# Attention scores over all 128 rows, two heads' scores in turn, and state space copies and tables in another order

## The chip, the cores and the metric

The kernel runs on one core of one Trainium2 chip. The metric is the device time of one launch in microseconds (us). Before the change the median of three runs is 2548.87 us (2544.2 to 2550.59).

## What is computed

One sequence of 512 positions with 1024 features, float32, goes through two layers of a first block and one layer of a second. Weights stay in float32, so every large product is done in split form: each operand is a high part and a low part, and a product is high·high + high·low + low·high.

The first block has three branches from one input projection: attention in a window of 128 positions (8 query heads, 2 key heads, 64 features a head, with sinks), a short convolution, and a state space model (32 groups of 16 channels, 64 states). The part of it that the change touches is this:

```python
s = jnp.einsum("bnqkgd,bnskd->bnkgqs", qb, kb) * (HEAD_DIM ** -0.5)
...
bu = jnp.einsum("blgh,gph->blgp", uf.astype(jnp.complex64), b_bar)
...
_, states = lax.associative_scan(combine, (a_elems, bu), axis=1)
...
y = jnp.einsum("blgp,ghp->blgh", states, c_c).real
```

The second block has a convolution branch with 31 taps and a differential attention: 8 heads, two causal softmaxes each, the second subtracted with a weight from the first.

```python
s = jnp.einsum('bqhd,bkhd->bhqk', qb, k, preferred_element_type=jnp.float32) * scale
s = jnp.where(mask[None, None], s, -jnp.inf)
...
a = probs(qb1, k1) - lam * probs(qb2, k2)
```

## The kernel before

**Storage and weights.** Intermediate tiles live in 78 slots of 128x512 that are handed out in the order in which they became free (`big` L338, `free` L352); the 8 PSUM banks are handed out the same way (`psum` L346). A tile that gets a slot waits until the last reader or writer of the tile before it is done, whatever engine that is. Weights come in units of 128x1024 through three raw buffers (`_fetch` L416), are split by ACT (high, L375) and DVE (low, L378) and are used in a fixed order. DMA requests go out on SP in program order. A product of eight such pieces is `fm` (L470), three matmuls a piece (`mm3` L457: lines L460, L461, L462).

**Lanes.** The main stream is a row of such products. Everything else is written as Python generators in lanes: after every third piece a tick gives each lane some steps (`beat` L464, `tick` L486), so pieces of attention, of the state space model and of the convolution are put between the main matmuls. Inside an engine the instructions then run in a fixed order.

**First block, attention** (`_att_block` L961). There are 4 query blocks and 2 key heads in each of 2 layers, so 16 calls. A call does four query heads, two for each half `e`. The keys stand twice in a tile of 128 rows, in rows 0 to 63 and in rows 64 to 127 (`kth` high, `ktl` low). The query tile `qs[e]` has the high part of the head in one half of the rows and its low part in the other half. So L976 over all 128 rows gives high·high + low·high, and L977 over the 64 rows of the high part adds high·low. L976 and L977 follow each other in turn, 4 of each in a call, 64 of each in all, into one bank; the scores are 256 columns wide, and 128 in the first query block.

**First block, state space model.** Four channel tiles `ct` in a layer. `ssm_tables` (L1093) builds the tables of one tile on POOL, for which it first asks for `bc` by a DMA (L1105); `ssm` (L1135) uses them on all engines and hands six slots back (L1223, L1224). L1102 holds a table back: those of tiles 0 and 1 until no table is outstanding, those of tiles 2 and 3 until at most one is. So table 1 is built only when tile 0 has used table 0. In layer 1 the first tables are started during the last products of layer 0. At the end of a tile, L1233 to L1242 bring the result from a PSUM bank into the slot `y` by 16 copies of 32x128: row block `i` of the output, and for each the four phases `t`, which stand in four row blocks of the bank and go to every fourth column. Copies of even `t` are ACT's (L375 in the profile), those of odd `t` DVE's (L1238).

**Second block, attention** (`_diff_block` L1654). There are 4 parts of 2 heads and 4 query blocks, 16 calls. `e` is the head of the part, and stands in one half of the 128 rows; `s` is the softmax. A call does, for each `e` and each `s`, three matmuls of 64 rows (`mm3` again: hence L460 to L462 with 64*128), a mask with its minimum on DVE (`masked` L532, L534) and an exponential on ACT. The scores are 128, 256, 384 or 512 columns wide by query block. There is a yield between the two heads. The calls go through a lane of width 2.

Of the kernel before, what the change touches and what calls it, by code (L numbers as in the profile page):

```python
# [11 lines left out]
AF = mybir.ActivationFunctionType  # L12
# [295 lines left out]
class Net:  # L308
# [652 lines left out]
    def _att_block(self, n, g, kth, ktl, qt, vv, ao, nsink, left, end):  # L961
        nc = self.nc
        while qt[n] is None:
            yield
        ts_ = slice(128 * n, 128 * n + 128)
        qs = qt[n][0]
        k0 = 1 if n == 0 else 0
        w = 256 - 128 * k0
        cols = slice(128 * (n - 1 + k0), 128 * (n + 1))
        nm = self.small("nm", (128, 4), bufs=3)  # L970
        pr = [self.big("pr", shape=(128, 2, 256)) for _ in range(2)]
        for e in range(2):
            ps = self.psum("sc", (128, 2, 256))
            rows = slice(64 * e, 64 * e + 64)
            for i in range(2):
                nc.tensor.matmul(ps[:, i, :w], qs[e][:, 2 * g + i], kth[g][:, cols], start=True, stop=False)  # L976
                nc.tensor.matmul(ps[:, i, :w], qs[e][rows, 2 * g + i], ktl[g][rows, cols], start=False, stop=True)  # L977
            for i in range(2):
                h = 2 * i + e
                self.masked(pr[i][:, e, :w], ps[:, i, :w], self.wmask[:, 128 * k0:], nm[:, h:h + 1],  # L980
                            nsink[:, 4 * g + h:4 * g + h + 1])
            self.free(ps)
        es = self.small("es", (128, 4), bufs=3)
        self.sub(es, nm, nsink[:, 4 * g:4 * g + 4])
        self.act(es, es, AF.Exp)
        sm = self.small("sm", (128, 4), bufs=3)
        for h in range(4):
            self.act(pr[h // 2][:, h % 2, :w], pr[h // 2][:, h % 2, :w], AF.Exp, scale=-1.0,
                     bias=nm[:, h:h + 1], accum_out=sm[:, h:h + 1])
        qt[n][1] -= 1  # L990
        if not qt[n][1]:
            self.free(qs)
        yield
        self.add(sm, sm, es)
        ri = self.small("ri", (128, 4), bufs=3)
        nc.vector.reciprocal(out=ri, in_=sm)
        for h in range(4):
            v = pr[h // 2][:, h % 2, :w]
            self.ts(v, v, ri[:, h:h + 1], ALU.mult)
        yield  # L1000
        pts = []
        for b in range(k0, 2):
            pt = self.psum("pT", (128, 4, 128))
            for h in range(4):
                nc.tensor.transpose(pt[:, h], pr[h // 2][:, h % 2, 128 * (b - k0):128 * (b - k0) + 128], self.ident)
            ph, pl = self.big("ph", F32R, (128, 4, 128)), self.big("pl", F32R, (128, 4, 128))
            self.split(ph, pl, pt)
            self.free(pt)
            pts.append((ph, pl, n - 1 + b))
        self.free(pr)  # L1010
        yield
        po = self.psum("po", (128, 4, 128))

        for i, (ph, pl, b) in enumerate(pts):
            v = vv[b // 2][:, b % 2, g].rearrange("p e d -> p (e d)")
            nc.tensor.matmul(po, v, ph, start=i == 0, stop=False)
            nc.tensor.matmul(po, v, pl, start=False, stop=i == len(pts) - 1)
            self.free(ph, pl)
        lo = self.big("lo", shape=(64, 4, 128))
        self.act(lo, po[64:128])  # L1020
        for h in range(4):
            rows = slice(64 * (h % 2), 64 * (h % 2) + 64)
            self.add(ao[2 * g + h // 2][rows, ts_], po[0:64, h], lo[:, h])
        self.free(po, lo)
        left[0] -= 1
        if not left[0]:
            end()
# [65 lines left out]
    def ssm_tables(self, L, ct, tabs):  # L1093

        gp = self.nc.gpsimd
        lr, li, fr, fi, rho, st = self.steps
        c4 = slice(4 * ct, 4 * ct + 4)

        def b4(ap, n):
            return ap[:, c4].unsqueeze(2).to_broadcast([128, 4, n])  # L1100

        while sum(t is not None for t in tabs.values()) > (1 if ct > 1 else 0):  # L1102
            yield
        bc = self.big("bc", shape=(128, 4, 4, 16))
        self.nc.sync.dma_start(out=bc, in_=self.A["bc"][L, ct].rearrange("p w (q h) -> p w q h", q=4))  # L1105
        bl = self.big("bl", shape=(128, 2, 4, 64))
        cl = self.big("cl", shape=(128, 2, 4, 64))

        def at(t, r, j):
            return t[:, r, j].rearrange("p (q h) -> p q h", q=4)  # L1110

        w1, w2 = self.small("s_w1", (128, 4, 16)), self.small("s_w2", (128, 4, 16))
        self.cmul(at(bl, 0, 3), at(bl, 1, 3), bc[:, 0], bc[:, 1], b4(fr, 16), b4(fi, 16), w1, w2, gp)
        for j in (2, 1, 0):
            self.cmul(at(bl, 0, j), at(bl, 1, j), at(bl, 0, j + 1), at(bl, 1, j + 1), b4(lr, 16), b4(li, 16), w1, w2, gp)
        pr, pi = bc[:, 2], bc[:, 3]
        for j in range(4):
            self.cmul(at(cl, 0, j), at(cl, 1, j), pr, pi, b4(lr, 16), b4(li, 16), w1, w2, gp)
            pr, pi = at(cl, 0, j), at(cl, 1, j)
        yield  # L1120
        er, ei, rt = (self.big(n, shape=(128, 4, 128)) for n in ("Er", "Ei", "R"))
        gp.memset(er[:, :, 0:1], 1.0)
        gp.memset(ei[:, :, 0:1], 0.0)
        gp.tensor_copy(out=rt, in_=b4(rho, 128))
        gp.memset(rt[:, :, 0:1], 0.0)
        xx = self.big("xx", shape=(128, 2, 4, 64))
        for k in range(7):
            n = 1 << k
            self.cmul(er[:, :, n:2 * n], ei[:, :, n:2 * n], er[:, :, 0:n], ei[:, :, 0:n],
                      b4(st[:, k, 0], n), b4(st[:, k, 1], n), xx[:, 0, :, :n], xx[:, 1, :, :n], gp)  # L1130
        self.free(xx)
        tabs[ct] = (bc, bl, cl, er, ei, rt)
        yield

    def ssm(self, L, ct, u, tabs, ys2):  # L1135
        nc = self.nc
# [16 lines left out]
        for i in range(4):  # L1153
            for j in range(4):
                o = uu[32 * j:32 * j + 32, i]
                s = u[32 * i:32 * i + 32, j::4]
# [16 lines left out]
        for r in range(2):  # L1173
            for e in range(2):
                s = hm[:, 2 * r + e:2 * r + e + 1]
# [5 lines left out]
        for r in range(2):  # L1181
            ps = self.psum("V", (128, 4, 128))
# [49 lines left out]
        y = self.big(f"y{ct}")  # L1232
        for i in range(4):  # L1233
            for t in range(4):
                o = y[32 * i:32 * i + 32, t::4]
                s = py[32 * t:32 * t + 32, i]
                if t % 2:
                    nc.vector.tensor_copy(out=o, in_=s)  # L1238
                else:
                    self.act(o, s)  # L1240
            if i == 1:
                yield  # L1242
# [3 lines left out]
        g = self.big("gelu")  # L1246
# [407 lines left out]
    def _diff_block(self, part, n, qk, vv, ya, left, done):  # L1654
        nc = self.nc
        while len(qk) < 4:
            yield
        w = 128 * (n + 1)
        tn = slice(128 * n, w)
        sm = self.small("dsm", (128, 2, 2), bufs=3)  # L1660
# [1 line left out]
        kap = self.small("dka", (128, 2), bufs=3)  # L1662
        ss = self.small("dss", (128, 2), bufs=3)
        rs = self.small("drs", (128, 2), bufs=3)
        pp = []
        for e in range(2):
            rows = slice(64 * e, 64 * e + 64)
            mx = self.small("dmx", (128, 2), bufs=4)
            p = [self.big("dp"), self.big("dp")]
            for s in range(2):  # L1670
                ps = self.psum("dsc")
                self.mm3(ps[:, :w], qk[s][0][rows, tn], qk[s][1][rows, tn],
                         qk[2 + s][0][rows, :w], qk[2 + s][1][rows, :w], True, True)
                self.masked(p[s][:, :w], ps[:, :w], self.cmask[:, 512 - w:], mx[:, s:s + 1])
                self.free(ps)
            for s in range(2):
                self.act(p[s][:, :w], p[s][:, :w], AF.Exp, scale=-1.0, bias=mx[:, s:s + 1], accum_out=sm[:, e, s:s + 1])
            pp.append(p)
            if e == 0:
                yield  # L1680
        nc.vector.reciprocal(out=ri, in_=sm)
        self.stt(kap, sm[:, :, 0], self.nlam, ri[:, :, 1], ALU.mult, ALU.mult)
# [1 line left out]
        for e in range(2):  # L1684
            p = pp[e]
# [133 lines left out]
```

## Time and profile before

| | |
|---|---|
| median of three runs | 2548.87 us |
| the profiled execution | 2549.26 us |
| its span, from the first to the last instruction | 2547.6 us |
| DVE busy | 1652.6 us (65%) |
| ACT busy | 1057.8 us (42%) |
| POOL busy | 333.7 us (13%) |
| mean granted clock of TensorE | 0.987 of full speed |

PE is TensorE's matmuls, PEld its weight loads, DVE VectorE, ACT ScalarE, POOL GpSimd, SP the engine that issues the DMAs. A matmul's duration in the rows holds its pipeline; what a matmul costs in a row of them is the distance between two starts. In the timeline the columns are the start, the duration, the engine, the line, the operation, the output from its inputs, the rows and columns of the weights, the shape of the moving operand, how many are merged, and in brackets the idle time of the engine just before and who ended it. In a table of stretches each row has the stretch, its length, the busy time of each engine with its instructions, the granted clock as a share of 2.4 GHz, the share of the DMA engines and what they moved. A clock of 0.50 is 1.2 GHz, the lower of its two levels.

### The profile page before, as it was taken

The numbers are of one execution on the slowest core, as the hardware profiler recorded it, in microseconds if no ns is written. First come the engines' busy times: TensorE is split into PE (matmuls) and PEld (weight loads), VectorE is DVE, ScalarE is ACT, GpSimd is POOL, SyncE is SP. The second block draws the span as 40 slices with busy tenths as digits, with TensorE's granted clock in tenths as the row PEclk, the third lists the DMA queues.
The fourth block names the chain that finished last, engine by engine and source line by source line (L and its number), as shares of the span: only waits on it lengthen the run. The fifth ranks groups of instructions, "written<-read, shape, count | busy, mean of one in ns | idle before, by whom it ended". The sixth has DMA issues, their size and how long they took to land. (4 is left out here: it accounts for less than half of the span.)

```text
span 2547.6 us, 32617 instructions
## 1 busy us (share of the span) xinstructions
PE 2478.0 (97%) x12280; PEld 2072.3 (81%) x12280; DVE 1652.6 (65%) x3086; ACT 1057.8 (42%) x1974; POOL 333.7 (13%) x826
## 2 busy tenths in 40 slices
PE   9999899999999999989999999999999989999997
PEld 7878788888888887878888788998888769988886
DVE  6887855444355488795577754689889776633445
ACT  5556543333233355553332222433444565633322
POOL 6554100000032074500000000000000000000001
PEclk9999999999999999999999999999999989999999
DMA  4211133222223311123366642333221113222322
GB/s 154 82 58 69 67 122 101 99 94 97 99 95 109 122 64 59 64 78 122 113 201 215 208 149 91 101 124 108 75 75 58 63 63 108 75 91 92 100 92 73
DMA packets 85566, 256.58 MB, mean 101 GB/s; under 512 B 9632, under 2 KB 13088, under 8 KB 85408
## 3 DMA queue, kind: packets, MB, share of 16 engines
q1 hardware_dynamic: 85408, 254.50, 29.4%
q8 instruction: 96, 1.57, 0.3%
q14 instruction: 62, 0.51, 0.1%
HBM read 248.18 MB, written 6.29 MB: 100 GB/s over the span
## 5 line engine op out<-in xcount | busy, mean ns | idle before, releaser
L460 PE MATMUL bank<-slot,wh 128*128 128x512 f32 x2680 | 1054.7, 395 | 14.7 <-ACT slot L375 10.1
L462 PE MATMUL bank<-slot,wl 128*128 128x512 f32 x2680 | 1050.3, 393 | 4.5 <-DVE wl L378 4.4
L461 PE MATMUL bank<-slot,wh 128*128 128x512 f32 x2680 | 1050.1, 392 | 0.0
L375 ACT ACTIVATE wh<-raw 128x1024 fp32r<-128x1024 f32 (+3 forms) x371 | 385.7, 1041 | 773.4 <-PE bank L461 480.4
L460 PEld LDWEIGHTS bank<-slot,wh 128*128 128x128 f32 x2680 | 506.7, 189 | 121.9 <-ACT slot L375 11.1
L462 PEld LDWEIGHTS bank<-slot,wl 128*128 128x128 f32 x2680 | 506.3, 189 | 115.9 <-DVE wl L378 8.1
L461 PEld LDWEIGHTS bank<-slot,wh 128*128 128x128 f32 x2680 | 506.6, 189 | 104.9 <-issue 0.9
L378 DVE TENSOR_TENSOR wl<-raw,wh 128x1024 fp32r<-128x1024 f32 (+3 forms) x371 | 451.6, 1218 | 184.4 <-ACT wh L375 181.8
L378 DVE TENSOR_TENSOR slot<-bank,slot 128x512 f32<-128x512 f32 (+4 forms) x340 | 198.3, 593 | 239.0 <-PE bank L462 209.1
L378 DVE TENSOR_TENSOR slot<-slot,slot 128x512 f32<-128x512 f32 (+4 forms) x492 | 295.0, 617 | 73.9 <-ACT slot L375 70.4
L375 ACT ACTIVATE slot<-slot 128x512 fp32r<-128x512 f32 (+4 forms) x384 | 207.9, 550 | 301.8 <-DVE slot L378 254.7
L375 ACT ACTIVATE slot<-bank 128x512 f32<-128x512 f32 (+7 forms) x388 | 177.1, 470 | 162.7 <-DVE slot L1238 47.3
L460 PE MATMUL bank<-slot,slot 128*128 128x256 f32 (+3 forms) x720 | 207.5, 298 | 3.1 <-ACT slot L375 3.1
L461 PE MATMUL bank<-slot,slot 128*128 128x256 f32 (+3 forms) x720 | 203.9, 290 | 3.7 <-DVE slot L378 3.7
L462 PE MATMUL bank<-slot,slot 128*128 128x256 f32 (+3 forms) x720 | 203.2, 288 | 0.0
L396 DVE SCALAR_TENSOR_TENSOR slot<-slot,slot 128x512 f32<-128x512 f32 (+1 forms) x184 | 125.5, 699 | 83.6 <-DMA slot<-in_wada_dram 59.2
L378 DVE TENSOR_TENSOR slot<-slot,bank 128x512 f32<-128x512 f32 (+1 forms) x112 | 68.4, 610 | 168.0 <-PE bank L462 167.2
L396 DVE SCALAR_TENSOR_TENSOR slot<-slot,cw,slot 128x493 f32<-128x493 f32 (+25 forms) x240 | 166.7, 733 | 1.6 <-ACT slot L375 0.9
L460 PEld LDWEIGHTS bank<-slot,slot 128*128 128x128 f32 (+1 forms) x720 | 135.6, 192 | 18.1 <-issue 7.1
L461 PEld LDWEIGHTS bank<-slot,slot 128*128 128x128 f32 (+1 forms) x720 | 136.3, 192 | 6.9 <-DVE slot L378 4.0
L462 PEld LDWEIGHTS bank<-slot,slot 128*128 128x128 f32 (+1 forms) x720 | 137.0, 192 | 1.3 <-issue 0.4
L461 PE MATMUL bank<-wl,slot 128*128 128x512 f32 (+1 forms) x256 | 93.6, 365 | 0.0
(189 smaller groups left out, 1944.6 us busy)
## 6 DMA issues: line engine op xcount, KB each, us to landing
raw<-in_w_dram SPq DMA_DIRECT2D x351, 512.0 KB, 3.3
slot<-in_wada_dram SPq DMA_DIRECT2D x96, 256.0 KB, 5.4
raw<-in_w_dram SPq DMA_DIRECT2D x48, 448.0 KB, 3.3
slot<-in_x_dram SPq DMA_DIRECT2D x16, 256.0 KB, 3.8
xd<-slot SPq DMA_DIRECT2D x16, 256.0 KB, 3.7
slot<-xd SPq DMA_DIRECT2D x16, 256.0 KB, 3.5
raw<-in_w_dram SPq DMA_DIRECT2D x9, 384.0 KB, 3.1
raw<-in_w_dram SPq DMA_DIRECT2D x8, 256.0 KB, 2.7
```

The source lines that it names most:

```text
L375: return self.nc.scalar.activation(out=out, in_=in_, func=func, scale=scale, **kw)
L378: return (eng or self.nc.vector).tensor_tensor(out=out, in0=a, in1=b, op=op)
L396: return self.nc.vector.scalar_tensor_tensor(out=out, in0=a, scalar=s, in1=b, op0=op0, op1=op1, **kw)
L460: t.matmul(ps, ah, bh, start=start, stop=False)
L461: t.matmul(ps, ah, bl, start=False, stop=False)
L462: t.matmul(ps, al, bh, start=False, stop=stop)
```

## The change

Four edits.

- In `_att_block` L977's product goes over all 128 rows, so that low·low is added as well.
- In `ssm_tables` all tiles have the same condition: a table may be built while one other is outstanding. This concerns table 1 alone.
- In `ssm` the 16 copies are dealt out by row block `i`: the four of blocks 0 and 2 to ACT, those of blocks 1 and 3 to DVE.
- In `_diff_block` the loops over head and softmax are exchanged: both heads of one softmax go together, into two banks, and their six matmuls alternate between the two halves of the rows. The masks of both come next, then the exponentials; the yield stands between the two softmaxes.

```diff
@@ _att_block
         for e in range(2):
             ps = self.psum("sc", (128, 2, 256))
-            rows = slice(64 * e, 64 * e + 64)
+
             for i in range(2):
                 nc.tensor.matmul(ps[:, i, :w], qs[e][:, 2 * g + i], kth[g][:, cols], start=True, stop=False)
-                nc.tensor.matmul(ps[:, i, :w], qs[e][rows, 2 * g + i], ktl[g][rows, cols], start=False, stop=True)
+                nc.tensor.matmul(ps[:, i, :w], qs[e][:, 2 * g + i], ktl[g][:, cols], start=False, stop=True)
@@ ssm_tables
-        while sum(t is not None for t in tabs.values()) > (1 if ct > 1 else 0):
+        while sum(t is not None for t in tabs.values()) > 1:
             yield
@@ ssm
-                if t % 2:
+                if i % 2:
                     nc.vector.tensor_copy(out=o, in_=s)
                 else:
                     self.act(o, s)
@@ _diff_block
-        pp = []
-        for e in range(2):
-            rows = slice(64 * e, 64 * e + 64)
-            mx = self.small("dmx", (128, 2), bufs=4)
-            p = [self.big("dp"), self.big("dp")]
-            for s in range(2):
-                ps = self.psum("dsc")
-                self.mm3(ps[:, :w], qk[s][0][rows, tn], qk[s][1][rows, tn],
-                         qk[2 + s][0][rows, :w], qk[2 + s][1][rows, :w], True, True)
-                self.masked(p[s][:, :w], ps[:, :w], self.cmask[:, 512 - w:], mx[:, s:s + 1])
-                self.free(ps)
-            for s in range(2):
-                self.act(p[s][:, :w], p[s][:, :w], AF.Exp, scale=-1.0, bias=mx[:, s:s + 1], accum_out=sm[:, e, s:s + 1])
-            pp.append(p)
-            if e == 0:
+
+        pp = [[self.big("dp"), self.big("dp")] for _ in range(2)]
+        mx = [self.small("dmx", (128, 2), bufs=4) for _ in range(2)]
+        for s in range(2):
+            ps = [self.psum("dsc") for _ in range(2)]
+            for i, (x, y) in enumerate(((0, 0), (0, 1), (1, 0))):
+                for e in range(2):
+                    rows = slice(64 * e, 64 * e + 64)
+                    nc.tensor.matmul(ps[e][:, :w], qk[s][x][rows, tn], qk[2 + s][y][rows, :w], start=i == 0, stop=i == 2)
+            for e in range(2):
+                self.masked(pp[e][s][:, :w], ps[e][:, :w], self.cmask[:, 512 - w:], mx[e][:, s:s + 1])
+            self.free(ps)
+            for e in range(2):
+                v = pp[e][s][:, :w]
+                self.act(v, v, AF.Exp, scale=-1.0, bias=mx[e][:, s:s + 1], accum_out=sm[:, e, s:s + 1])
+            if s == 0:
                 yield
```

## Rows read from the trace of the kernel before

**Rows 1.** The page's first part: the span, and TensorE's busy time.
```profile
span 2547.6 us, 32617 instructions
PE 2478.0 (97%) x12280; PEld 2072.3 (81%) x12280; DVE 1652.6 (65%) x3086; ACT 1057.8 (42%) x1974; POOL 333.7 (13%) x826
```

**Rows 2.** Busy time by stage: first block's two layers, plain products, second block's attention.
```profile
60.00:268.00 208.00, 199.70 (x984) 163.14 (x984) 162.69 (x368) 116.44 (x267) 109.09 (x290) 0.97 0.20 68
900.00:1105.00 205.00, 188.94 (x922) 154.36 (x920) 164.28 (x343) 117.07 (x272) 108.33 (x291) 0.95 0.19 63
1536.00:1600.00 64.00, 64.00 (x284) 53.01 (x283) 28.64 (x36) 18.73 (x24) 0.00 (x0) 1.00 0.30 95
1792.00:2035.00 243.00, 240.06 (x1273) 192.97 (x1272) 205.76 (x442) 117.53 (x287) 10.33 (x10) 1.00 0.19 64
2035.00:2180.00 145.00, 130.08 (x793) 111.18 (x792) 101.82 (x234) 90.64 (x222) 7.55 (x10) 0.94 0.27 93
```

**Rows 3.** The same table, of the stretches in which PE stands still.
```profile
150.00:180.00 30.00, 26.21 (x96) 19.26 (x96) 22.02 (x55) 14.98 (x36) 13.13 (x30) 0.83 0.15 52
256.00:280.00 24.00, 17.93 (x81) 14.31 (x80) 21.80 (x34) 11.68 (x28) 7.72 (x16) 0.86 0.13 44
970.00:1000.00 30.00, 23.86 (x94) 17.75 (x94) 23.83 (x55) 14.54 (x35) 10.85 (x21) 0.89 0.16 54
1088.00:1112.00 24.00, 15.88 (x88) 13.99 (x85) 22.10 (x38) 14.05 (x31) 0.10 (x1) 0.79 0.19 66
```

**Rows 4.** Line L976's matmuls: count and shapes.
```profile
L976 PE MATMUL bank<-slot,slot x64: 220/382/582, 82.5 to 1020.5; 128*128 128x256 f32 x48, 128*128 128x128 f32 x16
```

**Rows 5.** Timeline of PE in a call of the first block's attention.
```profile
122.47 0.38 PE L977 MATMUL bank<-slot,slot 64*128 64x256 f32 x1
...
123.10 0.38 PE L977 MATMUL bank<-slot,slot 64*128 64x256 f32 x1
```

**Rows 6.** Timeline of PE around three 64-row score groups, 256, 512 and 128 wide.
```profile
1815.36 0.28 PE L462 MATMUL bank<-slot,slot 128*128 128x256 f32 x1
...
1816.33 0.28 PE L461 MATMUL bank<-slot,slot 128*128 128x256 f32 x1
...
2006.60 0.39 PE L462 MATMUL bank<-slot,wl 128*128 128x512 f32 x1
...
2008.15 0.40 PE L461 MATMUL bank<-slot,wh 128*128 128x512 f32 x1
...
1800.35 0.40 PE L462 MATMUL bank<-wh,slot 128*128 128x512 f32 x1
1800.68 0.33 PE L461 MATMUL bank<-slot,slot 64*128 64x128 f32 x1
1800.69 0.32 PE L460 MATMUL bank<-slot,slot 64*128 64x128 f32 x1
...
1801.51 0.40 PE L461 MATMUL bank<-wl,slot 128*128 128x512 f32 x1
```

**Rows 7.** Timeline of ACT and POOL: the waits around tables 1 and 2.
```profile
89.60 0.29 POOL L378 TENSOR_TENSOR s_w<-slot,s_fr 128x64 f32<-128x64 f32 x1 [31.44 <-DMA slot<-in_bc_dram]
157.63 0.63 ACT L375 ACTIVATE slot<-slot 128x512 fp32r<-128x512 f32 x1 [5.70 <-POOL slot L378]
905.89 0.29 POOL L378 TENSOR_TENSOR s_w<-slot,s_fr 128x64 f32<-128x64 f32 x1 [60.42 <-DMA slot<-in_bc_dram]
979.41 0.63 ACT L375 ACTIVATE slot<-slot 128x512 fp32r<-128x512 f32 x1 [7.73 <-POOL slot L378]
```

**Rows 8.** Waits of ACT (total us, times, longest), and PE's longest idle time.
```profile
ACT slot L375 <- DVE slot L1238: 58.1, 47, 5.6
...
1099.10 0.56 PE L1228 MATMUL bank<-slot,slot 128*128 128x128 f32 x1 [8.12 <-DVE slot L1238]
```

**Rows 9.** A long wait of POOL for a slot; SP's waits at line L1105.
```profile
671.24 0.10 POOL L1123 MEMSET slot<- 128x4 f32 x1 [195.54 <-PE bank L461]
...
SPq L1105 <- DVE slot L378: 31.1, 3, 13.5
```

## The prediction

> **What bounds the kernel now.** The first part of the page says it at once: TensorE's matmuls are busy for 2478.0 of 2547.6 us, 97% [rows 1]. Busy is not yet at its peak, so the next view is the busy time by stage [rows 2]. A stage of plain products has 284 matmuls of 512 columns in 64 us, 0.225 us each at full clock; that is the pace to hold everything against (256 columns cost half, 0.113 us). The change touches four other stages: the first block's layers from 60 to 268 and from 900 to 1105 us, and the second block's attention from 1792 to 2035 and on to 2180 us. In the first three PE is busy for 96, 92 and 99% of the time, and DVE, the next engine, for 78, 80 and 85%. So a PE microsecond taken out there should mostly shorten the run, with not very much room before DVE is next. From 2035 to 2180 us PE is busy for 90% only: there chains of small steps set the pace too.
>
> Then I looked for where PE stands still in these stages. There are four patches [rows 3], two in each layer. PE is idle for 3.8, 6.1, 6.1 and 8.1 us in them, in order of time, and the granted clock falls to the lower of its two levels for part of each: a mean of 0.83 over 30 us is 10.2 us at half speed, of which at most 3.8 were idle, so 3.2 to 5.1 us of work are lost on top. Done likewise for the others, the patches cost 7.0 to 8.9 (150 to 180 us), 6.4 to 9.4 (256 to 280), 6.4 to 9.4 (970 to 1000) and 9.1 to 13.1 us (1088 to 1112).
>
> **First edit: first-block scores over 128 rows.** No matmul comes or goes; one in two grows from 64 to 128 rows. What to see: L976 and L977 in turn start 0.63 us apart for two, 0.315 us each [rows 5], where 256 columns cost 0.113 in a plain row [rows 2]. The pair changes the number of rows at each step, and each step pays. There are 64 of each line, 48 of them 256 wide [rows 4]. If all run on 128 rows, the 96 wide ones save 0.202 us each, 19.4 us. For the 32 narrow ones I read no distance and take half that saving, 3.2 us. Together 22.6 us, in equal parts in the two layers; more is excluded, as the plain pace is the floor, and the least is 0, if DVE takes the time up. Masks, exponentials, banks and weight loads are as many as before, so nothing new waits. I take three quarters, **17 us**, since the masks on DVE must keep up with an engine that is already at 78 to 80%.
>
> **Second edit: table 1 earlier.** The work on POOL is the same; it moves. Now POOL is idle for 31.4 us before 89.6 us and for 60.4 us before 905.9 us, both times until the `bc` of table 1 has landed, and then it builds tables 1 and 2 one after the other; some 68 and 74 us later an instruction at the head of ACT's queue, a split into a slot that POOL still works on, is let go after 5.7 and 7.7 us [rows 7]. That is the first patch of each layer: PE runs out of what ACT should have given it. With one table outstanding allowed, table 1 is built in the gap before (in layer 1 as early as layer 0's last products). A table is half of 74, 37 us of POOL. Table 2 may still start only where tables 1 and 2 start now, so POOL is done some 30 us sooner, before ACT's split arrives, and both waits should go. At stake are 7.0 to 8.9 plus 6.4 to 9.4, so 13 to 18 us, and the bounds are 0 and 18. What is late next there is DVE (22.0 of 30 us busy, [rows 3]), so I take **12 us**. What the move issues elsewhere: POOL's 37 us fall beside products in which DVE is little loaded (28.6 of 64 us in such a stage [rows 2]), which costs nothing as long as that cover lasts; two `bc` requests go ahead of weight requests on SP, at nothing as long as their slots are free (a rival, below). Table 3 still waits for tile 1 and stays where it is.
>
> **Third edit: copies by row block.** Still 8 copies on each engine. Now each is let go by the one before it on the other engine: ACT waits 47 times for L1238, 58.1 us in all, and PE's longest idle time, 8.12 us, ends on L1238 [rows 8]. Whatever else DVE has in its queue between two copies delays ACT, and with it the weight splits behind. In runs of four, 15 handovers become at most 3. The patches at stake are the second of each layer, 6.4 to 9.4 plus 9.1 to 13.1, middle 19 us; but they are the end of a chain through all engines, of which the copies are one link, and table 3 another. So the bounds are 0 (the chain ends as late) and 19 (the copies were all of it). I take the runs of four to follow each other rather than to overlap, because in the rows every copy waits, those of other row blocks too, and put in **7 us**. The Trainium skill (PSUM — Partial Sum Buffer, PSUM bank collisions raise a hardware error) says that two engines may be in one bank together only in different quadrants of 32 partitions. By that rule the old order, which changed the quadrant at each copy, could have overlapped and the new one can't, so this edit would give nothing and the sum would be 43 instead of 50; the 47 waits show that the old order did not overlap either.
>
> **Fourth edit: both heads in turn.** 192 matmuls of 64 rows, 64 groups of three now, 32 groups of six then. A group of three costs, from the last plain start before it to the second plain start behind it and less two plain distances, 0.97 - 0.226 = 0.74 us at 256 columns and 1.55 - 0.45 = 1.10 us at 512 [rows 6]; for 384 I take the middle, 0.92. This counts the extra start on the way in and out. What do six in turn cost? The kernel before shows it by chance: at 1800.68 and 1800.69 us two matmuls of different halves start together, and six of them, the groups of both heads at 128 columns, take 1.16 - 0.45 = 0.71 us [rows 6], no more than three at 256. So I take six for the price of three: 8 groups saved at each of three widths, 8 x (0.74 + 0.92 + 1.10) = 22 us; at 128 columns nothing, since some of these overlap already. The upper bound is 22; the lower is 0, if each change of half costs what rows 5 show for a change of rows: six at 0.33 are 2.0 us, two groups at 512 are 2.2. About two thirds of it lie before 2035 us, where PE is the bound, one third in the stage behind. I take three quarters of the first and two fifths of the second, **14 us**. Two banks are held at a time instead of one after the other, and freed in the same step; the banks go round in the same order, so I cost that at nothing, as long as the masks of both heads follow at once. The exponentials of the first head now stand behind the second head's mask: one mask later, in a lane of two calls, hidden by the main products.
>
> **The sum.** 17 + 12 + 7 + 14 = 50 us off the profiled execution's own 2549.3 us (span 2547.6 [rows 1], 1.7 around it; 0.4 above the median of the runs): **2499 us**. With every term in full, 22.6 + 18 + 19 + 22 = 82 us, it would be 2468.
>
> **The rivals.**
> - *DVE becomes the bound.* It stands at 78 to 85% in the stages and its queue has a fixed order. If no stage gets over the highest share seen, 85%, the stages end at 162.7/0.85 = 191, 164.3/0.85 = 193 and 205.8/0.85 = 242 us: 17 + 12 + 1, and 2 from the last stage, 32 us in all: 2517 us. For it: DVE's shares [rows 2]. Against it: it is 90% busy and more in the short patches [rows 3], and short waits there are not its own work. Chance 0.22.
> - *Everything lands.* The clock no longer falls, PE is the bound throughout: about 78 us, 2471 us. For it: PE at 96 and 99%. Against it: four patches would have to vanish. Chance 0.14.
> - *The halves don't overlap.* Then the fourth edit gives its lower bound, 0 instead of 14: 2513 us. The pair at 1800.68 speaks against it. Chance 0.05.
> - *The copies give nothing.* The runs of four still follow each other and the chain's end hangs on table 3: 0 instead of 7, 2506 us. For it: POOL still builds table 3 late. Against it: the 47 waits [rows 8]. The page's rule above would end here. Chance 0.05.
> - *Slower: SP stops on a table's slot.* The request for `bc` of table 1 now stands on SP ahead of weight requests, and SP does nothing else until its slot is free. Three raw buffers cover three units of 24 matmuls, 16 us. A longer stop stands in PE's time at full price, so one of over 16 + 50 = 66 us makes the kernel slower; of 100 us, 2499 + 84 = 2583 us. For it: a slot that POOL wanted at this very place, while layer 0 ends, came free 195.5 us late [rows 9]. Against it: the waits at L1105 so far are three, 13.5 us at most [rows 9], and the oldest free slot is taken first. Chance 0.06.
>
> **How the numbers follow.** My forecast has 0.45, with a range of its own from 2485 to 2512. The remaining 0.03 is for a kernel in which the gains cancel against new waits. Left out of 2475 to 2530 are the slower case, the cancelled gains and half of the case in which everything lands: under 0.2. A measurement can tell about 0.3%, 8 us, from no change. All cases but the last two are faster by more than that; a tail of the DVE case is not: faster 0.89, same 0.04, slower 0.07.
>
> **What would show it.** First edit: L976 and L977 both on 128 rows, starts about 0.12 us apart. Second: POOL busy soon after 58 us in layer 0 and before 905 us in layer 1, no wait of ACT for POOL near 155 and 975 us, and the granted clock at 1.00 in the first patch of each layer. Third: L1238's copies in runs of four, ACT's waits for them far below 58 us, PE idle less around the second patches. Fourth: starts of 64-row matmuls in pairs, and six in the time of three. I am wrong if DVE is idle less than before for the same gain (the first rival), if a request at L1105 holds SP up for more than 16 us, or if the 64-row starts stay 0.2 us and more apart.

## The result, and the profile after

The changed kernel takes **2515.82 us** (median of 4, 2514.38 to 2516.97) against 2548.20 of the kernel before on the same chip: a ratio of 0.9874, 95% interval 0.9857 to 0.9891, so 32 us less (28 to 36). The forecast was 2499, in a range from 2475 to 2530: the sign and the range held, the sum of 50 us was too large by a third of itself. The profiled execution took 2516.28 us.

The page's first part answers to [rows 1]: the share of TensorE rises by a point, DVE is no busier than it was.

```profile
span 2514.5 us, 32649 instructions
...
PE 2451.9 (98%) x12280; PEld 2065.7 (82%) x12280; DVE 1642.0 (65%) x3086; ACT 1056.9 (42%) x1974; POOL 331.1 (13%) x826
```

The table by stage (duration; busy time of PE, PEld, DVE, ACT, POOL; granted clock; DMA share; GB/s) answers to [rows 2]. DVE is at 84, 83 and 84% in the first three.

```profile
60.00:268.00 208.00, 198.63 (x1031) 168.61 (x1029) 174.84 (x388) 123.36 (x285) 105.86 (x270) 0.98 0.20 68
900.00:1105.00 205.00, 195.73 (x1012) 167.42 (x1011) 170.53 (x352) 123.01 (x280) 67.21 (x182) 0.98 0.20 68
1792.00:2035.00 243.00, 230.88 (x1198) 184.48 (x1197) 203.84 (x437) 129.66 (x320) 11.57 (x13) 0.97 0.19 65
2035.00:2180.00 145.00, 140.65 (x953) 126.59 (x952) 100.99 (x232) 88.59 (x218) 5.88 (x8) 0.98 0.28 97
```

Fixed windows mislead once the work inside them has moved. So I laid the start of the same plain matmul in the two traces side by side. Of the matmuls that use a split weight (`wh` or `wl`) the 1080th starts at 328.3 us before and 313.7 after: layer 0 gave 14.6. The 4320th, behind layer 1, starts 33.5 earlier (1141.4 and 1108.0): layer 1 gave 18.9. For the matmul at 2182.8, behind the second block's attention, it is 33.8 (2149.0 after). **All of the gain comes from the first block; the second block's attention gave nothing.**

What became of each edit shows in four places. First edit: L977 has 128 rows, and the four starts of a call are 0.12 us apart, as against 0.315 in [rows 5] (timeline of PE).

```profile
126.26 0.28 PE L977 MATMUL bank<-slot,slot 128*128 128x256 f32 x1
126.38 0.28 PE L976 MATMUL bank<-slot,slot 128*128 128x256 f32 x1
126.50 0.28 PE L977 MATMUL bank<-slot,slot 128*128 128x256 f32 x1
```

Second edit: the waits of [rows 7] are gone, and with them the first patch of each layer. PE is busy throughout there, at a clock of 1.00, where [rows 3] have 0.83 and 0.89 (table by window).

```profile
150.00:180.00 30.00, 30.00 (x159) 25.43 (x158) 26.85 (x71) 20.75 (x49) 0.00 (x0) 1.00 0.26 88
...
970.00:1000.00 30.00, 30.00 (x152) 25.41 (x151) 24.63 (x69) 23.02 (x55) 0.00 (x0) 1.00 0.21 71
```

But ACT now waits for POOL elsewhere, and PE stands still right behind two of these waits (timeline of ACT; in brackets the idle time before, and what ended it).

```profile
65.64 0.91 ACT L375 ACTIVATE slot<-slot,cst 128x256 f32<-128x256 f32 x2 [4.88 <-POOL slot L378]
...
119.73 0.91 ACT L375 ACTIVATE slot<-slot,cst 128x256 f32<-128x256 f32 x2 [6.61 <-POOL slot L378]
...
918.90 0.91 ACT L375 ACTIVATE slot<-slot,cst 128x256 f32<-128x256 f32 x2 [7.62 <-POOL slot L378]
```

PE idles 2.33 us before 122.05 and 3.40 before 924.19; that ACT's wait is behind it is read from the times, since the row names DVE. In layer 0 POOL now works on tables 0 and 1 in turn, an instruction of one and then of the other, so table 0 is done later: the wait at 65.64 is for it. A table has 16 instructions of the form `slot<-s_w,s_w`, and the last one for table 0 ends at 70.15 instead of 57.30. The two longer waits are for the third table in POOL's order, table 2: its last such instruction ends 0.04 us before ACT starts, at 119.69 (in layer 1 at 918.87). Before, it ended at 163.83 (timeline of POOL, before and after):

```profile
163.51 0.32 POOL L378 TENSOR_TENSOR slot<-s_w,s_w 128x64 f32<-128x64 f32 x1
...
119.38 0.31 POOL L378 TENSOR_TENSOR slot<-s_w,s_w 128x64 f32<-128x64 f32 x1
```

So that table is done 44 us sooner, but ACT's instruction behind it comes sooner too: the ninth of its form (`slot<-slot,cst`, 128x256) was the 177th of all that ACT does and is now the 124th. In all ACT waits 45.9 us for slots that POOL works on at L378; before it was 41.2. At 124 us of the kernel before, the changed kernel is 3.1 us *behind*.

Third edit: the copies run in fours, and DVE's begin where ACT's end, at 250.85 us. ACT's waits for them fall from 58.1 us, 47 times [rows 8], to 20.4 us, 13 times (timeline of ACT and DVE). The other link of the chain in layer 0 stays: just ahead of these copies ACT waits 7.76 us for POOL, and PE idles 5.34 us before 256.16.

```profile
249.27 1.58 ACT L375 ACTIVATE slot<-bank 32x128 f32<-32x128 f32 x4
...
250.88 1.58 DVE L1238 COPY slot<-bank 32x128 f32<-32x128 f32 x4 [5.45 <-ACT slot L375]
```

Fourth edit: the source now alternates the heads, the chip does not. TensorE still gets three matmuls of one head, then other work, then three of the other (timeline of PE). At 256, 384 and 512 columns this holds for nearly every group; at 128 some alternate, as some did before [rows 6].

```profile
1814.56 0.96 PE L1673 MATMUL bank<-slot,slot 64*128 64x512 f32 x3
...
1816.95 0.79 PE L1673 MATMUL bank<-slot,slot 64*128 64x384 f32 x3
...
1820.49 0.96 PE L1673 MATMUL bank<-slot,slot 64*128 64x512 f32 x3
```

The order of an engine's instructions is laid out when the program is built; of what the source issues in a row, the build may put the instructions apart, and here it kept each bank's three together.

### The profile page after: what moved, and what is told of

Its sections match the earlier page's. It is cut to its first block, busy times and chain, and to the rows that moved or that the text cites. A ratio compares the mean times of both kernels' runs of the same rounds, so it can differ in the third digit from the quotient of the medians.

```text
span 2514.5 us, 32649 instructions
## 1 busy us (share of the span) xinstructions
PE 2451.9 (98%) x12280; PEld 2065.7 (82%) x12280; DVE 1642.0 (65%) x3086; ACT 1056.9 (42%) x1974; POOL 331.1 (13%) x826
## 4 chain that ended last, share of the span: by engine, by line
PE 79%; DVE 6%; POOL 5%; DMA 5%; ACT 2%; issue 2%; SPq 0%; POOLq 0%; DVEq 0%; ACTq 0%
PE bank L460 25%; PE bank L461 24%; PE bank L462 24%; DMA slot<-in_wada_dram 4%; POOL slot L378 3%; POOL s_w L378 2%; DVE slot L378 2%; DVE wl L378 2%; ACT slot L375 2%; DVE slot L396 1%; PE bank L1673 1%; DMA raw<-in_w_dram 1%; PE bank L1705 1%; PE bank L1005 0%; PE bank L1184 0%
## 5 line engine op out<-in xcount | busy, mean ns | idle before, releaser
L460 PE MATMUL bank<-slot,wh 128*128 128x512 f32 x2680 | 1053.7, 394 | 13.1 <-ACT slot L375 7.7
L378 DVE TENSOR_TENSOR wl<-raw,wh 128x1024 fp32r<-128x1024 f32 (+3 forms) x371 | 451.1, 1216 | 189.3 <-ACT wh L375 186.0
L378 DVE TENSOR_TENSOR slot<-bank,slot 128x512 f32<-128x512 f32 (+4 forms) x340 | 197.7, 592 | 233.3 <-PE bank L462 199.9
L378 DVE TENSOR_TENSOR slot<-slot,slot 128x512 f32<-128x512 f32 (+4 forms) x492 | 292.1, 611 | 56.5 <-ACT slot L375 53.6
L375 ACT ACTIVATE slot<-bank 128x512 f32<-128x512 f32 (+6 forms) x388 | 176.9, 471 | 132.7 <-PE bank L462 47.9
L462 PE MATMUL bank<-slot,slot 128*128 128x256 f32 x656 | 184.8, 285 | 0.0
L461 PE MATMUL bank<-slot,slot 128*128 128x256 f32 x656 | 184.7, 286 | 0.0
L460 PE MATMUL bank<-slot,slot 128*128 128x256 f32 x656 | 183.2, 288 | 0.3 <-ACT slot L375 0.3
L378 DVE TENSOR_TENSOR slot<-slot,bank 128x512 f32<-128x512 f32 (+1 forms) x112 | 68.3, 610 | 168.3 <-PE bank L462 167.5
L396 DVE SCALAR_TENSOR_TENSOR slot<-slot,cw,slot 128x485 f32<-128x485 f32 (+28 forms) x240 | 166.3, 728 | 1.9 <-ACT slot L375 1.1
L460 PEld LDWEIGHTS bank<-slot,slot 128*128 128x128 f32 x656 | 124.7, 194 | 2.4 <-ACT slot L375 1.2
L461 PEld LDWEIGHTS bank<-slot,slot 128*128 128x128 f32 x656 | 125.9, 193 | 0.9 <-issue 0.4
L462 PEld LDWEIGHTS bank<-slot,slot 128*128 128x128 f32 x656 | 126.2, 193 | 0.4
L583 POOL TENSOR_TENSOR rstd<-nv,mhalf 128x2 f32<-128x2 f32 (+1 forms) x11 | 10.5, 953 | 634.4 <-DVE nv L393 634.4
```

The costliest lines, as they stand in the source:

```text
L375: return self.nc.scalar.activation(out=out, in_=in_, func=func, scale=scale, **kw)
L378: return (eng or self.nc.vector).tensor_tensor(out=out, in0=a, in1=b, op=op)
L396: return self.nc.vector.scalar_tensor_tensor(out=out, in0=a, scalar=s, in1=b, op0=op0, op1=op1, **kw)
L460: t.matmul(ps, ah, bh, start=start, stop=False)
L461: t.matmul(ps, ah, bl, start=False, stop=False)
L462: t.matmul(ps, al, bh, start=False, stop=stop)
```

## The experiments

**Each edit alone, on the kernel before** (the kernel before took 2551.65 us beside these four, and each gain below is one less the ratio, times that).

```diff
-nc.tensor.matmul(ps[:, i, :w], qs[e][rows, 2 * g + i], ktl[g][rows, cols], start=False, stop=True)
+nc.tensor.matmul(ps[:, i, :w], qs[e][:, 2 * g + i], ktl[g][:, cols], start=False, stop=True)
```

> The first edit alone, on the kernel before. Theory: a change of row count costs PE about 0.2 us at each step and PE is the bound here, so the 96 wide score matmuls give 0.2 us each: 15 to 20 us less, about 2530 us, half of it in each layer. Rival (the stage's end hangs on the chain through POOL's tables and DVE's copies, which this edit does not touch): the scores come earlier and wait longer, 10 us less at most, and the idle time of PE at 155 and 975 us grows by what the scores save.

Measured: 2531.78 us, ratio 0.9919 (0.9906 to 0.9932): 20.7 us less (17 to 24); in the trace 9.9 in layer 0 and 8.8 in layer 1. The theory holds. Of the rival a part is true: PE's idle time does grow, at 155 us from 2.69 to 5.23 and near 970 us from 6.13 to 9.53 (timeline of PE), so the scores do come early and wait; but most of the saving of 0.2 us each is kept for all that.

```profile
158.80 0.58 PE L976 MATMUL bank<-slot,slot 128*128 128x256 f32 x1 [5.23 <-DVE slot L378]
...
967.49 0.79 PE L1016 MATMUL bank<-slot,slot 128*128 128x512 f32 x1 [9.53 <-ACT slot L375]
```

```diff
-while sum(t is not None for t in tabs.values()) > (1 if ct > 1 else 0):
+while sum(t is not None for t in tabs.values()) > 1:
```

> The second edit alone, on the kernel before. Theory: table 1 is built between the pieces of table 0, so the waits of ACT for POOL near 155 and 975 us go, but waits of 5 to 8 us come 40 us earlier, at about 65, 120 and 919 us: the wait has moved, and the gain is 2 to 8 us, 2540 to 2546 us. Rival (the changed kernel's gain in the layers comes mainly from here, as predicted): 12 us less, 2536 us, and no wait over 3 us in either layer.

Measured: 2545.87 us, 0.9976 (0.9967 to 0.9985): 6.1 us less (4 to 8). The theory holds: the wait has moved. At 126 us this kernel is 6.0 us behind the kernel before, and only by 173 us is it 2.2 ahead.

```diff
-if t % 2:
+if i % 2:
```

> The third edit alone, on the kernel before. Theory: the handovers go, PE's idle time at the end of each layer shrinks by what the copies held it, 3 to 8 us less, 2540 to 2545 us. Rival (the end of the chain hangs on table 3 and on DVE, the copies are hidden): within 2 us of the kernel before, though ACT's waits for the copies fall from 58 to about 20 us.

Measured: 2551.20 us, 0.9994 (0.9984 to 1.0005): 1.5 us less, no change that can be told. ACT's waits for the copies did fall, to 23.4 us, 14 times, as the rival said: alone, the copies are hidden behind tables and scores that are late anyway.

```diff
-self.mm3(ps[:, :w], qk[s][0][rows, tn], qk[s][1][rows, tn],
-         qk[2 + s][0][rows, :w], qk[2 + s][1][rows, :w], True, True)
...
+for i, (x, y) in enumerate(((0, 0), (0, 1), (1, 0))):
+    for e in range(2):
+        rows = slice(64 * e, 64 * e + 64)
+        nc.tensor.matmul(ps[e][:, :w], qk[s][x][rows, tn], qk[2 + s][y][rows, :w], start=i == 0, stop=i == 2)
```

> The fourth edit alone, on the kernel before. Theory: the build issues the three matmuls of one head together, whatever order the source has, so TensorE does what it did: within 2 us of the kernel before, 2546 to 2550 us, groups of three at 0.74 to 1.1 us as before. Rival (two banks held at a time and the exponentials behind the second head's mask cost or give something): over 4 us in either direction, from 1792 us on.

Measured: 2547.23 us, 0.9986 (0.9978 to 0.9995): 3.6 us less (1 to 6). Of that the trace shows 1.5 behind 1792 us; the rest lies ahead of any line that the edit touches. So this is close to nothing, as expected. The four gains add up to 31.9 us; all together gave 32. That they agree so well is partly chance: most of the 3.6 us is not the edit's, and the third edit is worth more in company, as the next run shows.

**The changed kernel less one edit.**

```diff
-if i % 2:
+if t % 2:
```

> The changed kernel without the third edit (copies by column again). Theory: the copies are worth 1 to 2 us as they were alone, 2516 to 2518 us. Rival (with the other edits in, the copies set the end of each layer): 4 to 8 us slower than the changed kernel, 2520 to 2524 us, and an idle time of PE of 6 us and more near 1065 us.

Measured: 2522.65 us, 0.9889 (0.9873 to 0.9904), 7 us above the changed kernel's median, and 4 by the two ratios, whose intervals overlap; the traces below bear out the 7. The rival is right: with scores and tables out of the way, the copies set the end of each layer. ACT's waits are back at 56.7 us, 43 times, and so is PE's long idle time (waits of ACT; timeline of PE):

```profile
ACT slot L375 <- DVE slot L1238: 56.7, 43, 4.4
```
```profile
1072.73 0.77 PE L1228 MATMUL bank<-slot,slot 128*128 128x128 f32 x2 [7.42 <-DVE slot L1238]
```

Against the changed kernel the starts are 3.1 us late behind layer 0 and 7.1 behind layer 1.

```diff
-for i, (x, y) in enumerate(((0, 0), (0, 1), (1, 0))):
...
+self.mm3(ps[:, :w], qk[s][0][rows, tn], qk[s][1][rows, tn],
+         qk[2 + s][0][rows, :w], qk[2 + s][1][rows, :w], True, True)
...
```

> The changed kernel without the fourth edit (one head's scores after the other). Theory: the same time within 3 us, 2513 to 2520 us, as TensorE's groups of three are the same. Rival (the edit gave 4 us or more, and something else took it back): 2520 us and more.

Measured: 2517.71 us, 0.9871 (0.9854 to 0.9888): 2 us above the changed kernel's median, which can't be told from it.

**The alternation forced.**

```diff
+with self.tc.manual_schedule(engines={mybir.EngineType.PE}):
     for i, (x, y) in enumerate(((0, 0), (0, 1), (1, 0))):
         for e in range(2):
             rows = slice(64 * e, 64 * e + 64)
...
```

> The changed kernel, with the six score matmuls of both heads held on TensorE in the order of the source (head 0, head 1, head 0, ...). Theory: the fourth edit gave nothing because the build issued three of one head and then three of the other; forced, the two halves run beside each other, six take about the time of three (0.7 to 1.1 us), and the stage from 1792 us on ends 8 to 16 us earlier, 2500 to 2508 us. Rival 1 (the halves do not overlap, and each change of half costs as in the first block's old scores): six take 2 us, no gain or up to 10 us more, 2516 to 2526 us. Rival 2 (they overlap, but DVE's masks and the small steps set the pace there): six take the time of three and the time falls by less than 4 us.

Measured: 2515.69 us, 0.9865 (0.9850 to 0.9880): no different from the changed kernel. Yet the price is what the prediction took: **six cost what three cost.** The forced kernel's timeline, and its groups by form, beside the changed kernel's (last columns: busy us, mean ns):

```profile
1811.68 0.79 PE L1674 MATMUL bank<-slot,slot 64*128 64x384 f32 x6
...
1822.44 0.96 PE L1674 MATMUL bank<-slot,slot 64*128 64x512 f32 x6
```
```profile
L1674 PE MATMUL bank<-slot,slot 64*128 64x512 f32 x48 | 9.2, 433 | 0.0
...
L1674 PE MATMUL bank<-slot,slot 64*128 64x384 f32 x48 | 8.0, 396 | 0.0
```
```profile
L1673 PE MATMUL bank<-slot,slot 64*128 64x512 f32 x48 | 14.7, 429 | 0.0
...
L1673 PE MATMUL bank<-slot,slot 64*128 64x384 f32 x48 | 12.1, 371 | 0.0
```

With 256 columns (10.1 to 7.5) and 128 (7.1 to 6.6) that is 12.7 us off TensorE's busy time, and not one off the run. Where it went shows in the table by window, first the changed kernel, then the forced one; the sums are over 1560 to 2180 us.

```profile
1760.00:1850.00 90.00, 89.38 (x516) 74.42 (x515) 78.66 (x166) 40.27 (x98) 2.91 (x3) 1.00 0.16 54
1850.00:1900.00 50.00, 49.74 (x280) 40.44 (x278) 45.57 (x107) 25.82 (x69) 3.20 (x3) 1.00 0.21 74
1900.00:1950.00 50.00, 48.61 (x242) 39.05 (x242) 46.11 (x81) 22.71 (x53) 1.70 (x2) 1.00 0.25 85
...
sum 620.00, PE 603.53 PEld 518.17 DVE 498.09 ACT 306.35 POOL 22.04; mean PE 67.06 PEld 57.57 DVE 55.34 ACT 34.04 POOL 2.45
```
```profile
1760.00:1850.00 90.00, 88.19 (x524) 74.18 (x523) 82.55 (x175) 42.41 (x103) 4.42 (x4) 1.00 0.16 54
1850.00:1900.00 50.00, 45.54 (x260) 36.64 (x259) 45.40 (x105) 25.51 (x68) 1.81 (x2) 0.93 0.22 77
1900.00:1950.00 50.00, 49.76 (x256) 40.39 (x255) 47.26 (x91) 22.20 (x52) 2.09 (x2) 1.00 0.23 82
...
sum 620.00, PE 593.83 PEld 513.41 DVE 496.66 ACT 304.43 POOL 22.59; mean PE 65.98 PEld 57.05 DVE 55.18 ACT 33.83 POOL 2.51
```

TensorE is 9.7 us less busy in the same stretch and stands still for as much more, and the clock falls to 0.93 from 1850 to 1900. DVE is at 91 to 95% there (87 to 92% in the changed kernel). Its late masks hold a bank that a plain matmul wants (timeline of PE in the forced kernel), though of PE's 7.3 us idle from 1760 to 2000 us masks end only 2.8, and ACT 3.7. Later a chain that begins with a weight's transfer (6.08 us from 2069.09) leaves 4.23 us open:

```profile
1825.22 0.38 PE L460 MATMUL bank<-slot,slot 128*128 128x256 f32 x1 [1.81 <-DVE dmx L534]
...
1885.52 0.58 PE L1724 MATMUL bank<-cst,slot 128*128 128x128 f32 x2 [2.14 <-ACT slot L375]
...
2079.06 1.12 PE L1698 MATMUL bank<-cst,slot 128*128 128x128 f32 x4 [4.23 <-DVE slot L396]
```

Two suspects, then: DVE before 2000 us, or the small steps and weights behind it.

**Work taken off DVE.** First by moving the second block's rotation of queries and keys to POOL, in the changed and in the forced kernel.

```diff
-self.mul(a, a, tab(cos))
-self.add(a, a, b)
+self.mul(a, a, tab(cos), self.nc.gpsimd)
+self.add(a, a, b, self.nc.gpsimd)
...
```

> The changed kernel with the second block's rotation of queries and keys (16 products of 256 and 16 products and sums of 512 columns, some 17 us of DVE between 1760 and 2000 us) on POOL, which is idle there. It is the base for the next run. Theory: DVE is not quite the bound in this stage as the changed kernel stands, so 0 to 6 us less, 2510 to 2516 us. Rival (POOL is slower at it, and the scores wait for the rotated tiles): 3 to 10 us more.

> The kernel with forced alternation of the heads, and the rotation on POOL as in the run before. Theory: with the heads alternating DVE became the bound (97% busy from 1800 to 1850 us) and its late masks held the banks; with 17 us taken off DVE the forced order is worth 6 to 12 us against the run before, 2500 to 2508 us. Rival (the small steps behind 2000 us and the weights that arrive there set the end, whatever DVE does): the two runs differ by less than 3 us.

Measured: 2523.64 us (0.9891, 0.9876 to 0.9907) and 2524.73 (0.9899, 0.9881 to 0.9916): 8 us *more* than the changed kernel between the medians (4 by the ratios), and no difference between the two orders. This tells nothing of the two suspects, since it did not relieve DVE: from 1792 to 1850 DVE is busy for 53.95 and 53.23 of 58 us, as against 51.25 in the changed kernel. Why is told at the end. The other way is to leave work out: every second tap of the convolution, in the forced kernel.

```diff
+if j % 2:
     self.stt(acc[:, s:], us[i][:, :512 - s], self.cw[:, 31 * i + j:31 * i + j + 1], acc[:, s:], ALU.mult, ALU.add)
```

> The kernel with forced alternation of the heads, and every second tap of the second block's convolution left out (120 of 240 passes of DVE at about 0.73 us, some 88 us between 1560 and 2000 us), so the second block's convolution is incomplete. Theory: DVE, over 90% busy from 1792 to 1950 us, took what the forced order saved on TensorE, as its late masks held banks; with DVE below 80% there, TensorE's idle time before 2000 us goes and the forced order's 10 us show: 2500 to 2509 us. The changed kernel itself, with TensorE 98% busy before 2000 us, had at most 4 us to gain from a lighter DVE there. Rival (the small steps and the weights behind 2000 us set the end, whatever DVE does before): 2512 to 2518 us, and the idle time behind 2000 us grows by what was saved before.

Measured: 2494.67 us, 0.9773 (0.9757 to 0.9789), **21 us less than the forced kernel** between the medians (23 by the ratios), more than the theory's 7 to 16. The same windows:

```profile
1760.00:1850.00 90.00, 90.00 (x543) 75.33 (x542) 69.72 (x161) 46.10 (x115) 3.61 (x4) 1.00 0.20 71
1850.00:1900.00 50.00, 50.00 (x297) 41.60 (x296) 41.79 (x94) 26.24 (x68) 1.70 (x2) 1.00 0.16 53
1900.00:1950.00 50.00, 50.00 (x257) 40.44 (x256) 25.05 (x58) 23.78 (x60) 2.50 (x3) 1.00 0.21 74
```

PE never stands still from 1760 to 1950, and its clock stays up. A matmul that the forced kernel starts at 1894.5 starts 13.1 us earlier here, one at 2024.5 18.0 earlier, one at 2177.5 24.1 earlier. No TensorE work was taken out, so DVE's load is a large part of what kept the forced order from paying. How much of the 21 us the order gives and how much the lighter DVE would give without it stays open: the changed kernel with half the taps was not run. Its own idle time in these three windows is 0.62 + 0.26 + 1.39 = 2.3 us, but it starts the first of the three matmuls at 1888.3, ahead of the forced kernel, so of the 13.1 us there 6.2 only make up what the forced order had lost.

The other suspect is not cleared. The forced kernel enters this stage 2.8 us ahead of the changed one (1663.4 and 1666.2 for the same matmul), is 8.3 ahead at 2059.9, and 1.0 at 2177.5. What it had won by 2060 us it lost again behind it, where the 4.23 us stand and DVE is busy for 59% (2050 to 2100 us). These marks count main matmuls alone, and other work can lie on either side of them.

**The order of the tables on POOL.** First the whole of POOL in the order of the source:

```diff
-ctx.enter_context(tc.manual_schedule(engines={mybir.EngineType.SP}))
+ctx.enter_context(tc.manual_schedule(engines={mybir.EngineType.SP, mybir.EngineType.Pool}))
```

> The changed kernel, with POOL's instructions in the order of the source over the whole kernel, so that table 0 is built before table 1 instead of in turn with it. Theory: table 0 in turn with table 1 is what makes ACT wait at 65 to 70 us and moves PE's idle time to 122 and 924 us; in order, those waits go and 5 to 10 us more are gained, 2506 to 2511 us. Rival (the waits come from table 1 being on POOL at all at that time, or a later instruction of POOL now stands behind a table): the waits move again, within 4 us of the changed kernel or slower.

Measured: 2525.45 us, 0.9901 (0.9887 to 0.9916): 10 us more. The rival was right. A memset of the state space of tile 0 (L1219) now stands behind table 1, and ACT behind it (timelines of ACT and PE):

```profile
114.44 1.26 ACT L375 ACTIVATE slot<-s_dd 32x128 f32<-32x128 f32 x4 [12.41 <-POOL slot L1219]
```
```profile
118.68 0.80 PE L1016 MATMUL bank<-slot,slot 128*128 128x512 f32 x1 [8.32 <-ACT slot L375]
```

Then the tables alone in order, each behind the last instruction of the table before (`tab_last`), all else on POOL free:

```diff
+behind = self.tc.issue_after(self.tab_last.ins) if ct else contextlib.nullcontext()
+with behind:
     self.cmul(at(bl, 0, 3), at(bl, 1, 3), bc[:, 0], bc[:, 1], b4(fr, 16), b4(fi, 16), w1, w2, gp)
...
```

> The changed kernel with each table's instructions on POOL queued behind the last of the table before, and all other POOL instructions left free, so that the zeroing of the state space's matrix does not stand behind a table. Theory: table 0 is ready at about 57 us as before the change, ACT's waits for it at 65 and 70 us go, and PE's idle time at 122 us with them: 3 to 8 us less than the changed kernel, 2508 to 2513 us. Rival (in turn, the two tables filled each other's gaps, so that the second is now done later and ACT waits for that one): within 2 us or slower, and a wait of ACT for POOL of more than 6 us behind 110 us.

Measured: 2513.91 us, 0.9856 (0.9840 to 0.9871): 2 below the changed kernel, which can't be told. Table 0 is ready 12 us earlier (ACT's wait for it ends at 54.00), but the third table hardly is: it is begun at 91.22 as against 93.55, ACT waits 7.36 us for its last instruction of that form, until 117.45, and PE stands still for 4.9 us in all around that. In turn or one after the other, the two tables ahead of it are as much POOL time. None of the kernels with the whole computation beats the changed one by more than can be told.

## Why the prediction was right, and where it failed

- **First edit, 17 us of at most 22.6: too low by a little.** Alone it gave 20.7 (17 to 24). The step rows 4 times 0.202 us was right: in the medians of all starts a wide score matmul went from 0.313 to 0.120 us and a narrow one from 0.253 to 0.112, so 96 x 0.193 and 32 x 0.141, 23 us. What was lost of it shows as idle time of PE, which in the two windows of [rows 2] grew from 24.4 to 31.4 us; that DVE sets a limit, for which the quarter was taken off, is not shown, and DVE went on from 78 to 84% in layer 0 of the changed kernel.
- **Second edit, 12 us: half of it.** It gave 6.1. The step that failed was "POOL is done some 30 us sooner, before ACT's split arrives, and both waits should go". POOL was done sooner, by 44 us with the third table of layer 0, and the two waits went. But ACT's instruction arrived sooner as well, and two other waits came, of 6.61 and 7.62 us, 38 and 60 us earlier. I had moved POOL's work and left ACT's order where it was; the build moved that too. Nor had I asked who else was on POOL in the gap given to table 1: in layer 0 it was table 0, which came 13 us later.
- **Third edit, 7 us: right in company, nothing alone.** 1.5 us alone, and 7 on top of the others between the medians, 4 by the ratios. The copies follow each other, as taken (250.85 and 250.88); so the rule of the Trainium skill (PSUM — Partial Sum Buffer, PSUM bank collisions raise a hardware error), by which the edit was to give nothing, did not decide it. What paid was the handovers.
- **Fourth edit, 14 us: failed, at two steps.** The one that the text left out: that the source's order would be TensorE's order. That "the change doesn't do what it says" was not among the rivals; the kept groups of three show it at a glance. Of its own steps, "six for the price of three" was right (0.79 and 0.96 us), and "two thirds lie before 2035 us, where PE is the bound" was wrong: PE was 99% busy there, DVE 85%, and of the 10 us taken off PE nothing was left at the end: waits on DVE and ACT before 2000 us and the chain behind 2060 us took them. Forced, the edit was still worth nothing. One reading of [rows 6] was off: between 1800.35 and 1801.51 stand five 64-row matmuls, not six, as the first of the six had started at 1799.53; the forced kernel bears the price out all the same.
- **The rivals.** "DVE becomes the bound" gave 2517 and so the best number, by 17 + 12 + 1 + 2 us against 14.6 + 18.9 + 0 + 0. That is luck: as a mechanism it is shown in the second block alone, in part, and there for the forced order. In the first block it was not tested; the three single gains there add up to 28.3 us and together gave 33.5, which a ceiling shared by the edits would not let them do. SP did not stop on a table's slot: its waits at L1105 total 29.3 us, the longest 13.1. The rival "the halves don't overlap" is refuted by the forced kernel.
- The sum against the result: 50 predicted; 20.7 + 6.1 + 1.5 + 3.6 measured. The missing 18 us are 6 of the second edit and 10 of the fourth, and the third's 5.5 stand against 3.7 more of the first. The time lies outside the forecast's own range (2485 to 2512) and inside the whole one, which reached to 2530 for the sake of rivals that are not what happened: that much is luck.

The Trainium skill has a sentence that fits the fourth edit (TensorEngine Tiling (Array Packing), PSUM Bottleneck): tiling speeds up TensorE but not the emptying of PSUM, which may become the bottleneck after a fourfold speedup. The runs agree in part, at a twofold one: two masks of 0.68 us empty what six matmuls now fill in 0.96 us at 512 columns, and PE's waits on a mask from 1760 to 2000 us went from 1.3 to 2.8 us, which is not the whole of what was lost.

## What to carry to other kernels

An order in the source is a wish: before a gain rests on it, look up the order in which the engine gets the instructions, and where it differs, hold it there. Time taken off an engine that is 99% busy is gained only as far as the next engine, at 85 to 95%, and the chains behind it let it; say beforehand which work would have to go. Work that is moved into a gap shares it with what stands there already, the instruction that waits for it may move as well, and an edit that gives nothing alone can be worth 4 to 7 us once the waits in front of it are gone.

## What was not expected of the hardware

Products on POOL slow DVE down, but only some of its instructions. The rows are groups of DVE by form from 1792 to 1900 us, the changed kernel first, then the one with the rotation on POOL, and POOL's own (busy us, mean ns).

```profile
L378 DVE TENSOR_TENSOR wl<-raw,wh 128x1024 fp32r<-128x1024 f32 x10 | 12.2, 1221 | 0.3 <-ACT wh L375 0.3
...
L534 DVE CUSTOM_DVE_ANT_0 slot<-bank,slot 128x384 f32<-128x384 f32 x8 | 4.4, 554 | 1.1 <-PE bank L1673 0.7 <-PE bank L1705 0.4
...
L396 DVE SCALAR_TENSOR_TENSOR slot<-slot,cw,slot 128x484 f32<-128x484 f32 x2 | 1.4, 716 | 0.0
```
```profile
L378 DVE TENSOR_TENSOR wl<-raw,wh 128x1024 fp32r<-128x1024 f32 x8 | 11.9, 1489 | 1.2 <-ACT wh L375 1.2
...
L534 DVE CUSTOM_DVE_ANT_0 slot<-bank,slot 128x384 f32<-128x384 f32 x8 | 4.2, 552 | 0.0
...
L396 DVE SCALAR_TENSOR_TENSOR slot<-slot,cw,slot 128x484 f32<-128x484 f32 x2 | 3.4, 1688 | 0.0
...
L378 POOL TENSOR_TENSOR slot<-slot,slot 128x512 f32<-128x512 f32 x23 | 38.9, 1713 | 0.1
```

Some taps of the convolution take 1.69 us, as long as POOL's product (1.71), where 0.72 is usual; three that fall where POOL is idle take 2.27 together (at 1806.57). The weight split goes from 1.22 to 1.49; a mask that reads a bank keeps its 0.55. So the 17 us taken off DVE came back as longer instructions. The Trainium skill (SBUF — State Buffer, SBUF: two separate sides) states a rule that fits: DVE and GpSimd share a pair of ports as an exclusive lock, and an operation of DVE with two SBUF inputs contends for it against a GpSimd operation that reads SBUF; the taps and the split have two such inputs, the mask has one.
